# First layer's attention: value pieces traced ahead of transposes and scores

## The chip, the cores and the metric

The kernel runs on one core of a Trainium2 chip. A core has five engines with instruction streams of their own: TensorE (PE; its weight loads are listed apart, as PEld), VectorE (DVE), ScalarE (ACT), GpSimd (POOL) and SyncE (SP), which here issues the DMAs. Each engine runs its instructions in the order in which the program lists them; between engines, semaphores make an instruction wait for what it needs. Matrix products and transposes are written to PSUM, from where DVE and ACT read them; GpSimd works on SBUF only in this kernel.

The metric is the time of one execution on the device, in microseconds (us), as the median of several runs.

## What is computed

Two layers over 1024 latent tokens and 256 context tokens, model width 1024, 16 heads of 64. The first layer is a windowed attention in which four query heads share one key and value head, with rotary embedding and a sink logit per head; the second is a neighbourhood attention on a grid. Both have a gate path. The change lies in the first layer's attention. Cut to what matters:

```python
def block(bi):                       # one block of 128 queries; keys: 3 blocks + context
    s_lat = jnp.einsum('bqkgd,bjkd->bkgqj', qb, kb) * scale
    s_lat = jnp.where(mask, s_lat, NEG_INF)
    s_ctx = jnp.einsum('bqkgd,bckd->bkgqc', qb, kc) * scale
    p = jax.nn.softmax(jnp.concatenate([s_lat, s_ctx, s_sink], axis=-1), axis=-1)
    o = jnp.einsum('bkgqj,bjkd->bqkgd', p_lat, vb) + jnp.einsum('bkgqc,bckd->bqkgd', p_ctx, vc)
    return o.reshape(B, A_BLOCK, A_INNER)
...
y = (o * jax.nn.silu(g)) @ w_out
h = layer_norm(DEEPNORM_ALPHA * h + gate[:, None, :] * y, ln_g[i], ln_b[i])
```

The two context blocks attend to the context alone, and go through the same code with two key tiles instead of four or five.

## The kernel before

**Number format.** Products run on pairs: a value is kept as a high part (a cast) and a low part (the value minus its high part). A projection therefore takes three matmuls (L206 to L208), and the probabilities are stored as `pth` (high) and `ptl` (low).

**Units.** The first layer's attention runs over 8 head pairs `p`, 10 blocks `b` of 128 queries and 2 heads `h`: 160 sub-steps `k`. The two heads of a block form one unit `u`, with sub-steps 2u and 2u+1. Each sub-step has these pieces:

- S, the scores (`qkA`, L692): four matmuls into a PSUM tile "big" (L702, L703). `sm_first` follows: DVE adds the mask and takes the extreme (L315), POOL writes the sink's column (L320), ACT takes the exponential (L322).
- T, the transposes (`trA`, L716, with `sm_transpose`, L329): 2 to 5 transposes of 128 columns into another "big" tile (L334). ACT casts them to `pth` (L338), DVE computes `ptl` (L340). The same piece calls `sm_second` for the next sub-step: DVE's reciprocal (L326) and POOL's scaling (L327).
- V, the values (`pvA_fn`, L723), once per unit and in two halves: V1 multiplies with `pth` of both heads, V2 with `ptl` (L731). After V2 of an odd block the results of two blocks are evacuated: copies on ACT (L740), sums on DVE (L741), the product with the gate on POOL (L744), and at the last block of a pair of heads a store (L748; L746 for the last pair).

**Buffers.** PSUM has two "big" tiles (`psbig`, L95), used by scores and transposes alike, and four "one" tiles (`psone`, L98), used by projections and values. `pth` and `ptl` have two buffers each (`pt_tile`, L342), one per unit.

**Order.** `att_steps` (L750) writes the pieces out row by row. Row k holds T(k), S(k+3), and one half of a unit's values: in odd rows V1 of the unit that ends with sub-step k-2, in even rows V2 of the unit that ends with k-3. So rows 2u+3 and 2u+4 hold V1(u) and V2(u). `merge` (L282) spreads the projections of the gate and of the next head pair's queries between these pieces, in proportion to written costs (545 for T, 545 for S, 1090 / 2 for each half of V), and with a due number for V2 (`needA`, L791), which makes sure that the gate's part is there. Reductions, loads of keys and values, and the column sums of the modulation ("dots", L615, L616, L597) are inserted at fixed places of the list of pieces. For the last head pair the last six pieces are traced after the gates' transposes (L844 to L846).

The order in which pieces are traced is a priority for the planner that orders each engine's instructions; it also goes by when an instruction can be ready by its own estimate. `lift(n)` moves instructions n places ahead: 80 for `sm_first` and `sm_second` (LIFT_A), 60 for L340, 20 for L338. The second layer uses the same `att_steps` with whole value pieces (`split=False`).

Of the kernel before, what the change touches and what calls it, by code (L numbers as in the profile page):

```python
# [80 lines left out]
def build(tc, i, out):  # L81
# [44 lines left out]
    def lift(n):  # L126

        return tc.high_priority(n) if n else nullcontext()
# [196 lines left out]
    def sm_second(s):  # L325
        nc.vector.reciprocal(s.rs, s.sum)  # L326
        nc.gpsimd.tensor_scalar(s.t[:, : s.w], s.t[:, : s.w], s.rs, 1.0, ALU.mult, ALU.mult)  # L327
# [422 lines left out]
    def att_steps(subs, qk, st, tr, pv, last_of_unit, costs, need, ahead, rise, split=False):  # L750

        seq = []
        n = len(subs)
        for k in range(-ahead, n + 2 + split):
            row = []

            def t_piece(k=k):
                if k + 1 < n:
                    with lift(rise(k)):
                        sm_second(st[k + 1])  # L760
                if k >= 0:
                    tr(k)

            def s_piece(k=k):
                qk(k + ahead)

            def v_piece(k=k):
                pv(k - 2)

            def v_first(k=k):  # L770
                pv(k - 2, 0)

            def v_second(k=k):
                pv(k - 3, 1)

            if -1 <= k < n:
                row.append((costs[0] if k >= 0 else 0.0, t_piece, 0))
            if k + ahead < n:
                row.append((costs[1], s_piece, 0))
            if split and 0 <= k - 2 < n and last_of_unit(k - 2):  # L780
                row.append((costs[2] / 2, v_first, 0))
            elif split and k - 3 >= 0 and last_of_unit(k - 3):
                row.append((costs[2] / 2, v_second, need(k - 3, k + ahead)))
            elif not split and k - 2 >= 0 and last_of_unit(k - 2):
                row.append((costs[2], v_piece, need(k - 2, k + ahead)))
            seq.append(row)
        return seq

# [2 lines left out]
    def needA(k, kq):  # L791
# [5 lines left out]
        return G7_AT[c] if p == 7 else 8 * (c + 1)  # L797

    rowsA = att_steps(
        subsA, qkA, stA, trA, lambda k, x: pvA_fn(*subsA[k][:2], x), lambda k: subsA[k][2] == 1,  # L800
        (545, 545, 1090), needA, AHEAD_A, lambda k: LIFT_A, True,
# [6 lines left out]
    for p in range(8):  # L808
# [6 lines left out]
        if p < 7:  # L815
            n = len(att)
# [272 lines left out]
    for p in range(8):  # L1089
# [6 lines left out]
        fillB += gp  # L1096
        g_done.append(len(fillB))
    rowsB = att_steps(
        subsB, qkB, stB, trB, lambda k: pvB_fn(subsB[k][0], subsB[k][1]), lambda k: subsB[k][2] == 1,
        (545, 545, 1310), lambda k, kq: g_done[subsB[k][0] // 2], AHEAD_B, lambda k: LIFT_B if k >= BARE_B else 0,  # L1100
# [86 lines left out]
    for j in range(4):  # L1187
        t = ob.tile([P, D], F32, name=f"vec{j}")
# [136 lines left out]
```

## Time and profile before

| | us |
|---|---|
| median of 3 runs | 1452.0 |
| lowest and highest run | 1451.5, 1457.64 |
| profiled execution | 1452.42 |
| its span | 1450.4 |

The span is the time from the first to the last instruction of the profiled execution; 2.0 us of that execution lie around it. The profile's page lists the busy time of each engine and the chain of work that ended last, followed back from the last instruction. The windows give the busy time of each engine in a stretch of the span. The waits say how long an engine stood still and which instruction ended that. The timeline lists instructions by their start, with the idle time before them in brackets. A matmul's end is modelled, and matmuls overlap, so PE counts as busy where short stalls may hide.

### The profile page before, as it was taken

The page shows a single profiled execution, that of the slowest core. Times are in us where ns is not written, and L with a number is a line of the kernel's source. Part 1 is how long each engine was busy: PE and PEld are TensorE (multiplying, and loading weights), DVE is VectorE, ACT ScalarE, POOL GpSimd, SP SyncE. Part 2 cuts the span into 40 slices and gives each one's busy share as a digit, 9 for nine tenths or more (in the row PEclk, how much of TensorE's full clock was granted, in tenths as well). Part 3 has the DMA queues.
Part 4 walks back from the last instruction along what each step waited for, and adds up shares of the span by engine and source line. Part 5 has one row for each costly group of instructions (what it writes and reads, how often), then busy time and mean ns, then how long its engine had stood idle before and what let it go on. Part 6 is the DMA issues. An engine that isn't in the chain of part 4 may idle for free.

```text
span 1450.4 us, 25150 instructions
## 1 busy us (share of the span) xinstructions
PE 1392.4 (96%) x8816; PEld 1214.8 (84%) x8816; DVE 991.1 (68%) x2220; ACT 733.6 (51%) x1565; POOL 632.2 (44%) x779
## 2 busy tenths in 40 slices
PE   9999999999999999999999999999999999988995
PEld 5887898888888888788898889888988898877774
DVE  4658888878888789566433765555565555677788
ACT  4336776677676777332222545444454445466300
POOL 0326666666666657233301323333233323354664
PEclk9999999999999999999999999999999999999998
DMA  9472114123122124434287565554555464563543
GB/s 370 164 233 83 56 53 131 45 77 101 68 70 62 56 69 130 134 127 141 75 238 227 145 185 171 142 156 151 162 152 171 122 185 137 144 196 97 146 115 93
DMA packets 117229, 195.05 MB, mean 134 GB/s; under 512 B 9328, under 2 KB 57840, under 8 KB 117104
## 3 DMA queue, kind: packets, MB, share of 16 engines
q1 hardware_dynamic: 117104, 193.45, 43.8%
q8 instruction: 70, 1.15, 0.3%
q14 instruction: 55, 0.45, 0.1%
HBM read 141.51 MB, written 51.90 MB: 133 GB/s over the span
## 4 chain that ended last, share of the span: by engine, by line
PE 72%; DVE 11%; DMA 5%; issue 5%; ACT 4%; POOL 3%; SPq 0%; DVEq 0%; ACTq 0%; POOLq 0%
PE pj L207 9%; PE pj L206 9%; PE pj L208 9%; PE T_B L334 4%; PE T_A L334 4%; PE pvB L1064 3%; PE pvA L731 3%; PE pv L240 3%; PE pv L241 3%; PE pv L242 3%; PE S_A L702 2%; PE S_B L1033 2%; PE yA L419 2%; PE yA L418 2%; PE yA L417 2%
## 5 line engine op out<-in xcount | busy, mean ns | idle before, releaser
L327 POOL TENSOR_SCALAR s_B<-s_B,rs_B 128x640 f32<-128x640 f32 (+1 forms) x128 | 102.1, 798 | 305.7 <-DVE rs_B L326 285.6
L206 PE MATMUL pj<-uBh,wh 128*128 128x512 f32 (+1 forms) x448 | 176.2, 393 | 0.0
L207 PE MATMUL pj<-uBl,wh 128*128 128x512 f32 (+1 forms) x448 | 170.1, 380 | 0.0
L208 PE MATMUL pj<-uBh,wl 128*128 128x512 f32 (+1 forms) x448 | 169.8, 379 | 0.0
L322 ACT ACTIVATE s_A<-s_A,m_A 128x641 f32<-128x641 f32 (+2 forms) x160 | 119.5, 747 | 88.6 <-DVE m_A L315 74.3
L322 ACT ACTIVATE s_B<-s_B,m_B 128x640 f32<-128x640 f32 (+1 forms) x128 | 102.9, 804 | 119.9 <-DVE m_B L315 118.9
L340 DVE TENSOR_TENSOR pt_B<-T_B,pt_B 128x640 fp32r<-128x640 f32 (+1 forms) x128 | 100.9, 788 | 81.0 <-ACT pt_B L338 80.4
L162 POOL TENSOR_TENSOR wl<-wr,wh 128x512 fp32r<-128x512 f32 x64 | 87.8, 1372 | 147.7 <-ACT wh L160 143.1
L327 POOL TENSOR_SCALAR s_A<-s_A,rs_A 128x640 f32<-128x640 f32 (+2 forms) x160 | 126.8, 793 | 57.8 <-DVE rs_A L326 55.5
L315 DVE CUSTOM_DVE_ANT_0 s_A<-S_A,msk,nsk 128x640 f32<-128x640 f32 (+2 forms) x160 | 123.5, 774 | 34.0 <-PE S_A L703 17.7
L206 PE MATMUL pj<-uAh,wh 128*128 128x512 f32 (+1 forms) x384 | 140.0, 365 | 0.0
L207 PE MATMUL pj<-uAl,wh 128*128 128x512 f32 (+1 forms) x384 | 137.6, 358 | 0.0
L208 PE MATMUL pj<-uAh,wl 128*128 128x512 f32 (+1 forms) x384 | 137.3, 358 | 0.0
L340 DVE TENSOR_TENSOR ptl_A<-T_A,pth_A 128x640 fp32r<-128x640 f32 (+2 forms) x160 | 114.0, 712 | 15.2 <-PE pvA L731 7.1
L338 ACT CAST pt_B<-T_B 128x640 fp32r<-128x640 f32 (+1 forms) x128 | 84.4, 659 | 67.4 <-PE T_B L334 66.8
L334 PE MATMUL T_A<-ident,s_A 128*128 128x128 f32 x672 | 101.0, 275 | 12.0 <-DVE m_A L315 8.5
L334 PEld LDWEIGHTS T_A<-ident,s_A 128*128 128x128 f32 x672 | 77.2, 140 | 40.0 <-issue 17.0
L315 DVE CUSTOM_DVE_ANT_0 s_B<-S_B,bias 128x640 f32<-128x640 f32 (+1 forms) x128 | 100.3, 784 | 10.7 <-PE S_B L1034 9.7
L338 ACT CAST pth_A<-T_A 128x640 fp32r<-128x640 f32 (+2 forms) x160 | 96.4, 603 | 16.6 <-PE T_A L334 13.8
L334 PE MATMUL T_B<-ident,s_B 128*128 128x128 f32 x608 | 88.2, 274 | 12.5 <-DVE pt_B L340 8.5
L208 PEld LDWEIGHTS pj<-uBh,wl 128*128 128x128 f32 x448 | 84.3, 188 | 16.9
L334 PEld LDWEIGHTS T_B<-ident,s_B 128*128 128x128 f32 x608 | 70.0, 140 | 29.8 <-issue 11.8
(219 smaller groups left out, 3900.1 us busy)
## 6 DMA issues: line engine op xcount, KB each, us to landing
kB<-kdB SPq DMA_DIRECT2D x64, 320.0 KB, 5.3
gw<-in_wadaT SPq DMA_DIRECT2D x48, 256.0 KB, 2.8
vdB<-st SPq DMA_DIRECT2D x20, 512.0 KB, 3.1
vB<-vdB SPq DMA_DIRECT2D x16, 640.0 KB, 5.0
wada<-in_wadaC SPq DMA_DIRECT2D x16, 512.0 KB, 9.6
kdB<-st SPq DMA_DIRECT2D x16, 512.0 KB, 3.0
qdB<-st SPq DMA_DIRECT2D x16, 512.0 KB, 3.7
qB<-qdB SPq DMA_DIRECT2D x32, 256.0 KB, 4.5
```

Of the source, the lines that this page charges most:

```text
L162: e.tensor_tensor(lo, r, f32(hi), ALU.subtract)
L206: mm(pt[:, :n], hi[:, sl], rh, start=kt == 0, stop=False)
L207: mm(pt[:, :n], hi[:, sl], rl, start=False, stop=False)
L208: mm(pt[:, :n], lo[:, sl], rh, start=False, stop=kt == KT - 1)
L240: mm(pt, lh, hi[:, sl], start=kt == 0, stop=False)
L241: mm(pt, lh, lo[:, sl], start=False, stop=False)
L315: nc.vector.tensor_tensor_reduce(outp, sc, in1, scale, init if init is not None else 3e38, ALU.add, ALU.min, accum_out=s.m)
L322: nc.scalar.activation(s.t[:, :n], s.t[:, :n], AF.Exp, bias=s.m, scale=-1.0, accum_out=s.sum)
L327: nc.gpsimd.tensor_scalar(s.t[:, : s.w], s.t[:, : s.w], s.rs, 1.0, ALU.mult, ALU.mult)
L334: nc.tensor.transpose(tp[:, k * P : (k + 1) * P], s.t[:, src * P : (src + 1) * P], ident)
L338: nc.scalar.copy(pt.hi[:, :n, hl, :], tv)
L340: nc.vector.tensor_tensor(pt.lo[:, :n, hl, :], tv, f32(pt.hi[:, :n, hl, :]), ALU.subtract)
```

## The change

In `att_steps` the pieces of a row are collected and put together in another order. With `split` (the first layer) a row with a half of the values now has that half first, then T, then S; before it was T, S, values. Without `split` (the second layer) the order stays T, S, values. Pieces, costs and due numbers are the same.

```diff
-            if -1 <= k < n:
-                row.append((costs[0] if k >= 0 else 0.0, t_piece, 0))
-            if k + ahead < n:
-                row.append((costs[1], s_piece, 0))
+            t = [(costs[0] if k >= 0 else 0.0, t_piece, 0)] if -1 <= k < n else []
+            s = [(costs[1], s_piece, 0)] if k + ahead < n else []
+
             if split and 0 <= k - 2 < n and last_of_unit(k - 2):
-                row.append((costs[2] / 2, v_first, 0))
+                row += [(costs[2] / 2, v_first, 0)] + t + s
             elif split and k - 3 >= 0 and last_of_unit(k - 3):
-                row.append((costs[2] / 2, v_second, need(k - 3, k + ahead)))
+                row += [(costs[2] / 2, v_second, need(k - 3, k + ahead))] + t + s
             elif not split and k - 2 >= 0 and last_of_unit(k - 2):
-                row.append((costs[2], v_piece, need(k - 2, k + ahead)))
+                row += t + s + [(costs[2], v_piece, need(k - 2, k + ahead))]
+            else:
+                row += t + s
             seq.append(row)
```

Over the whole list this exchanges the two halves' places: the sequence T, S, V1, T, S, V2 becomes V1, T, S, V2, T, S, so that the half of a unit stands where the half before it stood.

## The prediction

> **What bounds the kernel now.** I read the page first, then the windows, then the waits of each engine inside the first layer's attention, then the timeline around single waits.
>
> ```profile
> span 1450.4 us, 25150 instructions
> PE 1392.4 (96%) x8816; PEld 1214.8 (84%) x8816; DVE 991.1 (68%) x2220; ACT 733.6 (51%) x1565; POOL 632.2 (44%) x779
> PE 72%; DVE 11%; DMA 5%; issue 5%; ACT 4%; POOL 3%; SPq 0%; DVEq 0%; ACTq 0%; POOLq 0%
> ```
>
> TensorE is busy 96% of the span and is 72% of the chain that ended last. It runs one stream in a fixed order, so time comes back only where that stream stands still. The windows (columns: stretch, its length, then busy us of PE, PEld, DVE, ACT, POOL, clock, DMA share, GB/s) show where that is:
>
> ```profile
> 140.00:590.00 450.00, 432.90 (x2818) 379.36 (x2817) 370.69 (x895) 317.05 (x718) 293.56 (x420) 1.00 0.24 76
> 1000.00:1200.00 200.00, 199.94 (x1362) 183.65 (x1361) 117.39 (x282) 97.24 (x204) 61.60 (x74) 1.00 0.55 159
> ```
>
> The first layer's attention lies in the first stretch: PE is idle 450.00 - 432.90 = 17.1 us there, with DVE at 82% and the clock granted in full. In the second layer PE is idle 0.06 us of 200, so what the first layer gives back should arrive at the end undiminished: the tail is the same PE stream begun earlier. The change can win at most about these 17.1 us, unless stalls are hidden inside matmuls shown as busy. What PE waits for in the attention (window 120 to 600; us in total, times, longest):
>
> ```profile
> PE T_A L334 <- DVE m_A L315: 8.3, 13, 1.6
> PE S_A L702 <- DVE ptl_A L340: 5.1, 7, 1.2
> PE S_A L703 <- DVE ptl_A L340: 1.8, 6, 0.3
> ```
>
> Transposes and scores share two PSUM tiles ("big"). A score waits until L340, the low half of an earlier transpose, has read its tile (6.9 us, 13 times); a transpose waits until L315, the score's reduction, has read its own (8.3 us, 13 times). Both releasers are on DVE.
>
> **The change part by part.** Nothing is added or removed: 80 first and 80 second value pieces, the transposes and the scores stay. In the repeating order T, S, V, T, S, V each value piece takes the place that the previous one had, one step sooner against T and S. What this unties is a buffer. `ptl` has two buffers, a unit is two sub-steps, and unit u+2 takes the buffer of unit u. In row 2u+4 the old order runs T(2u+4), S(2u+7), and only then V2(u), the last reader of that buffer; so L340 of T(2u+4) must wait for a value piece that comes after the next score. In the new order V2(u) precedes T(2u+4). The trace shows the knot (DVE's waits, then the timeline):
>
> ```profile
> DVE ptl_A L340 <- PE pvA L731: 7.1, 14, 1.2
> ```
>
> ```profile
> 299.93 0.71 PE L334 MATMUL T_A<-ident,s_A 128*128 128x128 f32 x5
> ...
> 301.53 0.69 ACT L338 CAST pth_A<-T_A 128x640 fp32r<-128x640 f32 x1
> ...
> 301.77 0.63 PE L731 MATMUL pvA<-ptl_A,vA 128*128 128x256 f32 x4
> ...
> 302.84 0.69 DVE L609 SCALAR_TENSOR_TENSOR gh<-gth,gh 128x512 f32<-128x512 f32 x1 [0.29 <-POOL s_A L327]
> 303.45 0.82 DVE L340 TENSOR_TENSOR ptl_A<-T_A,pth_A 128x640 fp32r<-128x640 f32 x1
> ...
> 303.94 0.69 ACT L338 CAST pth_A<-T_A 128x640 fp32r<-128x640 f32 x1
> ...
> 304.32 0.44 PE L702 MATMUL S_A<-kA,qA 128*128 128x384 f32 x1 [0.53 <-DVE ptl_A L340]
> ...
> 308.51 0.76 PE L731 MATMUL pvA<-ptl_A,vA 128*128 128x256 f32 x5
> ```
>
> The cast that L340 needs ended at 301.53 + 0.69 = 302.22; the value piece ended at 302.40; L340 started at 303.45, behind L609, and the score stood 0.53 us. Without the value piece the planner can put L340 ahead of L609; it would end at about 303.4, before the score's turn at 303.8. The longest such wait has the same shape:
>
> ```profile
> 154.58 0.38 PE L334 MATMUL T_A<-ident,s_A 128*128 128x128 f32 x2
> ...
> 155.44 0.37 ACT L338 CAST pth_A<-T_A 128x256 fp32r<-128x256 f32 x1
> ...
> 156.06 0.93 DVE L470 TENSOR_TENSOR ra<-ra,rb 128x512 f32<-128x512 f32 x1
> 156.10 0.76 PE L731 MATMUL pvA<-ptl_A,vA 128*128 128x256 f32 x5
> ...
> 157.67 1.15 DVE L658 TENSOR_TENSOR qA<-ra,qA 64x512 fp32r<-64x512 f32 x1 [0.28 <-ACT qA L657]
> ...
> 158.85 0.42 DVE L340 TENSOR_TENSOR ptl_A<-T_A,pth_A 128x256 fp32r<-128x256 f32 x1
> ...
> 159.33 0.39 PE L702 MATMUL S_A<-kA,qA 128*128 128x256 f32 x1 [1.20 <-DVE ptl_A L340]
> ```
>
> The cast is over at 155.81, the value piece at 156.86, and L340 comes third on DVE, at 158.85. **Term 1:** 0.53 + 1.20 = 1.7 us back.
>
> The eleven other score waits are 6.9 - 1.7 = 5.2 us. Of L702's seven, five are left with 5.1 - 1.73 = 3.4 us, 0.67 each, and they look like this one:
>
> ```profile
> 338.97 0.76 PE L731 MATMUL pvA<-ptl_A,vA 128*128 128x256 f32 x5
> ...
> 339.92 0.38 ACT L338 CAST pth_A<-T_A 128x256 fp32r<-128x256 f32 x1
> ...
> 340.81 0.69 DVE L658 TENSOR_TENSOR qA<-ra,qA 64x512 fp32r<-64x512 f32 x1
> ...
> 341.53 0.42 DVE L340 TENSOR_TENSOR ptl_A<-T_A,pth_A 128x256 fp32r<-128x256 f32 x1
> ...
> 342.01 0.39 PE L702 MATMUL S_A<-kA,qA 128*128 128x256 f32 x1 [0.67 <-DVE ptl_A L340]
> ```
>
> Here the value piece was over at 339.73 but the cast only at 340.30, and L658 went first on DVE. The buffer did not hold L340 directly; only the order that the planner wrote, perhaps with the buffer in mind, did. The bounds are 0 and 5.2 us. **Term 2:** half, 2.6 us back. The Trainium skill, "Perfetto Trace Analysis", section Optimization Strategy, says that the same gap repeated on the engine that should be saturated can mean too little PSUM or SBUF for the next tile. By it these repeated waits are two PSUM tiles too few, which an order does not cure; the sum would be 2.6 us worse. The trace bears half of that out: they do repeat at 0.67 us, but DVE work of another kind stands between.
>
> The transposes' 8.3 us have mixed causes. One of the larger:
>
> ```profile
> 249.97 1.44 DVE L615 CUSTOM_DVE_ANT_0 gj<-gw,gh 128x512 f32<-128x512 f32 x1 [0.54 <-DMA gw<-in_wadaT]
> ...
> 252.38 0.74 PE L334 MATMUL T_A<-ident,s_A 128*128 128x128 f32 x5 [1.16 <-DVE m_A L315]
> ```
>
> L615, waiting for a load, was ahead of L315. The change does not touch that, but it gives back DVE's 7.1 us of blocked waiting, which now delays whatever is behind L340, L315 among it. The bounds are 0 and 8.3. **Term 3:** a quarter, 2.1 us, since the one shown is of another kind.
>
> What moves along: each second piece of an odd block brings two L740 copies on ACT, two L741 on DVE, the multiply L744 on POOL, and seven times a store on SP's queue:
>
> ```profile
> L741 DVE TENSOR_TENSOR otmp<-pvA,otmp x78: 394/417/420, 138.7 to 591.2; 64x256 f32<-64x256 f32 x78
> L744 POOL TENSOR_TENSOR gA<-otmp,gA x39: 729/737/1227, 141.5 to 591.6; 128x256 f32<-128x256 f32 x39
> L748 SPq DMA_DIRECT2D ogd<-gA x7: 326/327/327, 179.6 to 544.5; - x7
> ```
>
> POOL is busy 293.56 of 450 us and nothing soon reads the stores: cost nothing, covered by POOL's 35% of idle time; uncovered, 0.74 us each. On DVE there is no such cover: if L741 steps in front of L315 just when a transpose needs the tile, it costs 0.42 us each time, between 0 and 40 x 0.42 = 16.7 us (one delay for each of 40 pairs of blocks). L315 is lifted by 80 places and L340 by 60, L741 by none. **Term 4:** near the low end, one such delay, 0.4 us lost.
>
> The new wait: V1(u) now heads row 2u+3 and PE's stream behind it, T and S, waits if the cast of T(2u+1) is late. For the odd transpose whose cast ends at 304.63 the first piece takes the place that now begins at 308.51: 3.9 us of slack. Cost nothing; if casts slipped beyond that, each would hold PE by the excess.
>
> The ends: the last six pieces are traced after the gate transposes. In the new order T(158) falls behind them. Nearest row, the one wait there:
>
> ```profile
> PE yA L417 <- ACT gates L366: 0.9, 1, 0.9
> ```
>
> **Term 5:** between -0.9 and +0.9, taken at 0.4 lost. Sum: 1.7 + 2.6 + 2.1 - 0.4 - 0.4 = 5.6 us. The profiled execution took 1452.42 us, span 1450.4 and 2.0 around it; 1452.4 - 5.6 = **1446.8 us**. The median of the three runs, 1452.0, is 0.4 us below the profiled one, less than any term.
>
> **The rivals.** (a) *More comes back.* Weight loads wait longer for L340 than matmuls do:
>
> ```profile
> PEld S_A L702 <- DVE ptl_A L340: 9.2, 18, 1.4
> PEld S_A L703 <- DVE ptl_A L340: 4.1, 6, 0.7
> ```
>
> If all 9.2 + 4.1 = 13.3 us goes, the time is 1452.4 - 13.3 = 1439.1 us; it lasts only if transposes do not then wait on L315 instead. Against it: some of it is hidden under matmuls still draining. The Trainium skill, "Perfetto Trace Analysis", section Identifying the Most-Contended Engine, calls matmul busy time a bad measure and takes the weight loads' share instead; by it PE has 450 - 379.36 = 70.6 us of room in this stretch, not 17.1. The back-to-back PE rows of the second layer (199.94 of 200) do not settle which is right. (b) *Nothing to measure.* The eleven waits are held by cast and queue, and the transposes' by loads: only Term 1 arrives, 1450.7 us; or the planner, which orders by readiness, already ran the pieces so and nothing changes, 1452.4. (c) *Slower.* The value evacuation, traced ahead, comes before the score's reduction on DVE: L741 in front of L315, the transposes wait 0.42 us at each. All 40 pairs give 16.7 us, less Term 1: 1452.4 + 16.7 - 1.7 = 1467.4. It decides from (7.3 + 1.7) / 0.42 = 21 pairs of 40. For it: DVE is 82% busy and transposes wait for L315 already. Against it: L315 is lifted by hand.
>
> **How the numbers follow.** 0.5% of 1452 is 7.3 us, about what a measurement of this kernel can tell from no change, so faster means below 1444.7 and slower above 1459.3. Forecast (1444.7 to 1450): 0.50. Rival (a): 0.26, all faster. Rival (b): 0.14, all within. Rival (c): 0.10, of which 0.07 beyond 21 pairs and 0.03 within. So faster 0.26, within 0.50 + 0.14 + 0.03 = 0.67, slower 0.07. The range runs from 1439 (rival (a), with the part above that value) to 1456 (rival (c) with 13 pairs: 5.4 - 1.7 = 3.7 us lost); it leaves out perhaps 0.08 on either side.
>
> **What would show it.** Right: DVE's waits of L340 for L731 (7.1 us, 14 times) nearly gone; scores waiting for L340 at 4 us or less from 6.9; transposes' waits for L315 at 6 to 7 us; PE's busy time from 140 to 590 unchanged in kind; span about 1444.8. Rival (b): the first goes and the second stays at 5 us. Rival (a): the second is nil and PE's idle time in the attention falls below 8 us. Rival (c): the transposes' waits for L315 rise past 15 us, with L741 running just ahead of L315. I am wrong altogether if PE waits for the cast L338 at value pieces, or if the second layer, whose trace order stays, loses or wins time of its own.

## The result and the profile after

The changed kernel takes 1462.7 us (median of four runs, 1460.8 to 1466.7) against 1452.0 before: a ratio of 1.0074, 95% interval 1.0058 to 1.0089. It is 10.8 us slower; 1446.8 was forecast. The profiled execution took 1462.72 us, with a span of 1460.9. Ratios here go by the fast runs alone and are not always the quotient of the medians shown (for a_tv0, below, they differ by some 0.001); one slow run of a_s0, at 1527.03 us, is left out of its median.

The page of the changed kernel (busy time of the engines, then the engines' shares of the chain that ended last):

```profile
span 1460.9 us, 25125 instructions
PE 1394.7 (95%) x8815; PEld 1221.4 (84%) x8816; DVE 990.4 (68%) x2220; ACT 734.0 (50%) x1565; POOL 634.3 (43%) x779
PE 62%; DVE 16%; ACT 6%; issue 6%; DMA 5%; POOL 4%; SPq 0%; DVEq 0%; ACTq 0%; POOLq 0%
```

The engines do the same work as before, but DVE has 16% of the chain instead of 11%. The windows of the changed kernel, with the start of the attention first (columns as in the prediction):

```profile
100.00:120.00 20.00, 16.75 (x89) 14.34 (x88) 13.40 (x34) 11.60 (x25) 7.40 (x13) 0.83 0.65 185
140.00:590.00 450.00, 427.18 (x2768) 376.84 (x2767) 366.29 (x887) 312.75 (x709) 293.69 (x419) 1.00 0.24 75
1000.00:1200.00 200.00, 199.94 (x1347) 182.88 (x1346) 118.30 (x284) 97.87 (x204) 62.95 (x74) 1.00 0.55 159
```

and the one of these stretches of the kernel before that has not been shown:

```profile
100.00:120.00 20.00, 19.12 (x119) 16.31 (x119) 13.81 (x33) 11.90 (x26) 8.36 (x13) 1.00 0.69 190
```

Between 140 and 590 PE is busy 427.2 us instead of 432.9, and 2768 matmuls start there instead of 2818. The second layer is untouched, 199.94 us of 200 in both. What PE waits for in the first layer's attention (120 to 610) in the changed kernel:

```profile
PE T_A L334 <- DVE ptl_A L340: 10.3, 15, 3.1
PE T_A L334 <- DVE m_A L315: 4.9, 9, 1.5
PE S_A L702 <- DVE ptl_A L340: 3.1, 3, 1.1
PE pvA L731 <- ACT pth_A L338: 1.7, 3, 0.8
```

The two waits that the prediction spoke of did become smaller: scores for L340 from 6.9 us to 3.1, transposes for L315 from 8.3 to 4.9. In their place stands one that the kernel before does not have at all: transposes that wait for L340, the low half of the transposes *before* them, 10.3 us. The value piece is no longer what L340 waits for. DVE's two longest waits in the changed kernel (120 to 610):

```profile
DVE rs_A L326 <- ACT s_A L322: 38.5, 57, 1.2
DVE ptl_A L340 <- ACT pth_A L338: 24.4, 50, 1.2
```

and the rows for these in the kernel before:

```profile
DVE rs_A L326 <- ACT s_A L322: 21.1, 43, 1.0
...
DVE ptl_A L340 <- ACT pth_A L338: 4.0, 9, 0.7
```

L340 for L731, 7.1 us before, is gone; L340 now comes to its turn early and stands waiting for the cast, six times as long as before. The timeline shows how that reaches PE. This is the change from the first head pair to the second, in the changed kernel; the values are those of the context blocks, the transposes those of block 0 of the next pair:

```profile
168.03 0.63 PE L334 MATMUL T_A<-ident,s_A 128*128 128x128 f32 x4
168.41 0.47 PE L206 MATMUL pj<-uAh,wh 128*128 128x512 f32 x1
...
169.31 0.44 PE L702 MATMUL S_A<-kA,qA 128*128 128x384 f32 x1
169.37 0.83 ACT L322 ACTIVATE s_A<-s_A,m_A 128x641 f32<-128x641 f32 x1 [1.55 <-POOL s_A L320]
...
169.99 0.40 PE L731 MATMUL pvA<-pth_A,vA 128*128 128x256 f32 x2
...
170.32 0.59 ACT L338 CAST pth_A<-T_A 128x512 fp32r<-128x512 f32 x1
...
170.94 0.69 DVE L340 TENSOR_TENSOR ptl_A<-T_A,pth_A 128x512 fp32r<-128x512 f32 x1 [0.45 <-ACT pth_A L338]
...
171.77 0.63 PE L334 MATMUL T_A<-ident,s_A 128*128 128x128 f32 x4 [0.68 <-DVE ptl_A L340]
```

and the same pieces in the kernel before:

```profile
166.74 0.60 PE L334 MATMUL T_A<-ident,s_A 128*128 128x128 f32 x4
166.80 0.83 ACT L322 ACTIVATE s_A<-s_A,m_A 128x641 f32<-128x641 f32 x1 [0.92 <-DVE m_A L315]
167.09 0.42 PE L702 MATMUL S_A<-kA,qA 128*128 128x384 f32 x1
...
167.75 0.59 ACT L338 CAST pth_A<-T_A 128x512 fp32r<-128x512 f32 x1
...
169.11 0.63 PE L334 MATMUL T_A<-ident,s_A 128*128 128x128 f32 x4
...
169.30 0.69 DVE L340 TENSOR_TENSOR ptl_A<-T_A,pth_A 128x512 fp32r<-128x512 f32 x1 [0.33 <-ACT th L275]
```

Before, the next transposes (169.11) start ahead of the L340 of the last ones (169.30): they take a tile that a *score* has left. In the changed kernel they wait for that L340: they take the tile of the last *transposes*. Counted in the programs, 21 of the 160 transposes took their tile over from transposes before the change, 83 after it. And between T and S there now stand projections (168.41 to 169.31), where S followed T at once before.

Nobody meant to move the projections. `merge` deals them out by place in the list, in proportion to the costs summed up so far, and a head pair's list now begins with a value piece instead of a transpose. (What is inserted at fixed places of the list, the column sums and the loads of keys and values, shifts against the pieces too.) Counted in the program as mean matmul time (us) between the pieces:

| | S to V | V to T | T to S |
|---|---|---|---|
| before | 0.51 | 0.65 | 0.18 |
| changed | 0.54 | 0.28 | 0.57 |

The largest single loss, in the changed kernel:

```profile
377.88 0.75 PE L731 MATMUL pvA<-ptl_A,vA 128*128 128x256 f32 x5
...
379.52 0.69 DVE L615 CUSTOM_DVE_ANT_0 gj<-gw,gh 128x512 f32<-128x512 f32 x1 [3.21 <-DMA gw<-in_wadaT]
...
380.77 0.82 DVE L340 TENSOR_TENSOR ptl_A<-T_A,pth_A 128x640 fp32r<-128x640 f32 x1
...
381.75 0.74 PE L334 MATMUL T_A<-ident,s_A 128*128 128x128 f32 x5 [3.12 <-DVE ptl_A L340]
```

Here DVE stands before L615 for a load, L340 is behind it, and the transposes are right behind the value piece with nothing in between.

Against the kernel before, the fifth product with the gate (L744) of the eight head pairs starts 1.1, 1.0, 3.7, 1.9, 7.6, 7.4, 9.8 and 9.9 us later. The loss comes in steps, the largest of them (5.7 us) in the pair with the wait at 381.75. The waits of PE that the profile lists from 120 to 610 rise only from 19.7 us to 22.3; the rest is hidden behind matmuls shown as busy. The starts of PE's matmuls show it. Take the distance from each matmul to the next, less the median distance behind the same kind of matmul in the kernel before, and add this up from the first score to the last value piece: it is 37.6 us before and 48.6 in the changed kernel, which is about the whole loss. Transposes right behind a value piece have 3.5 us of it before and 16.8 after; together with those behind a projection they have 19.0 and 30.2.

### The profile page after: what moved, and what is told of

It reads as the page before. It is cut to its first block, busy times and chain, and to the rows that moved or that the text cites. A ratio compares the mean times of both kernels' runs of the same rounds, so it can differ in the third digit from the quotient of the medians.

```text
span 1460.9 us, 25125 instructions
## 1 busy us (share of the span) xinstructions
PE 1394.7 (95%) x8815; PEld 1221.4 (84%) x8816; DVE 990.4 (68%) x2220; ACT 734.0 (50%) x1565; POOL 634.3 (43%) x779
## 4 chain that ended last, share of the span: by engine, by line
PE 62%; DVE 16%; ACT 6%; issue 6%; DMA 5%; POOL 4%; SPq 0%; DVEq 0%; ACTq 0%; POOLq 0%
PE pj L207 7%; PE pj L206 7%; PE pj L208 7%; PE T_B L334 4%; PE pvB L1065 3%; DVE s_A L315 3%; PE T_A L334 3%; PE pv L240 3%; PE pv L241 3%; PE pv L242 3%; PE S_B L1034 2%; DVE ptl_A L340 2%; PE yA L418 2%; PE yA L417 2%; PE yA L419 2%
## 5 line engine op out<-in xcount | busy, mean ns | idle before, releaser
L327 POOL TENSOR_SCALAR s_B<-s_B,rs_B 128x640 f32<-128x640 f32 (+1 forms) x128 | 102.3, 800 | 304.8 <-DVE rs_B L326 284.9
L340 DVE TENSOR_TENSOR pt_B<-T_B,pt_B 128x640 fp32r<-128x640 f32 (+1 forms) x128 | 100.9, 789 | 81.0 <-ACT pt_B L338 80.4
L206 PE MATMUL pj<-uAh,wh 128*128 128x512 f32 (+1 forms) x384 | 147.0, 383 | 0.0
L327 POOL TENSOR_SCALAR s_A<-s_A,rs_A 128x640 f32<-128x640 f32 (+2 forms) x160 | 124.6, 780 | 49.7 <-DVE rs_A L326 45.4
L340 DVE TENSOR_TENSOR ptl_A<-T_A,pth_A 128x640 fp32r<-128x640 f32 (+2 forms) x160 | 114.1, 713 | 28.2 <-ACT pth_A L338 27.6
L315 DVE CUSTOM_DVE_ANT_0 s_A<-S_A,msk,nsk 128x640 f32<-128x640 f32 (+2 forms) x160 | 123.1, 771 | 13.2 <-PE S_A L703 10.7
L315 DVE CUSTOM_DVE_ANT_0 s_B<-S_B,bias 128x640 f32<-128x640 f32 (+1 forms) x128 | 100.4, 785 | 10.3 <-PE S_B L1035 9.4
```

Source lines behind the costliest of these rows:

```text
L206: mm(pt[:, :n], hi[:, sl], rh, start=kt == 0, stop=False)
L315: nc.vector.tensor_tensor_reduce(outp, sc, in1, scale, init if init is not None else 3e38, ALU.add, ALU.min, accum_out=s.m)
L340: nc.vector.tensor_tensor(pt.lo[:, :n, hl, :], tv, f32(pt.hi[:, :n, hl, :]), ALU.subtract)
```

## The experiments

All ratios are against the kernel before, on the same chip, whose median lay between 1451.9 and 1452.3.

**DVE's order.** In the program L340 stood behind the score reduction L315 of sub-step k+3 for 135 of 160 transposes before, and for 72 after. Was that order the cause? Both kernels were made to have L340 behind that L315:

```diff
-        with lift(60 if a else 0):
-            nc.vector.tensor_tensor(pt.lo[:, :n, hl, :], tv, f32(pt.hi[:, :n, hl, :]), ALU.subtract)
+        def low():
+            with lift(60 if a else 0):
+                return nc.vector.tensor_tensor(pt.lo[:, :n, hl, :], tv, f32(pt.hi[:, :n, hl, :]), ALU.subtract)
+        return low
...
             def s_piece(k=k):
                 qk(k + ahead)
+                if split and k in lowA:
+                    with tc.issue_after(st[k + ahead].red.ins):
+                        lowA.pop(k)()
```

> The changed kernel, with one thing more: on VectorE the low half (L340) of transposes k is queued behind the score reduction (L315) of sub-step k+3, everywhere. The values stay first. Theory Q (the change lets the planner put L340 ahead of the score reduction on VectorE, where it waits for the cast and holds back the reduction): VectorE's idle time before L340 for the cast falls from 24.4 us to under 8, and the time falls by 6 us or more, to 1457 or below. Theory D (VectorE stands in front of loads for the modulation sums): the time stays at 1460 to 1465. Theory V (the values' place in TensorE's stream is itself what costs): it stays at 1460 to 1465.

> The kernel before, with the same rule on VectorE (L340 behind the score reduction of k+3), which already held for 135 of 160 there. Theory Q: little moves, 1449 to 1455. Theory V: as Q; then a_late stays above this one by 8 to 11 us, where theory Q has them within 4 us.

The changed kernel with this order (a_late) took 1462.3 us, ratio 1.007 (1.0055 to 1.0085); the one before (b_late) 1454.5, 1.0016 (1.0006 to 1.0026). DVE's order alone is not the cause, though the two kernels lie 7.8 us apart instead of 10.8: a_late's waits of PE and DVE show the stall under another name (its L707 is L703 of the others).

```profile
PE T_A L334 <- DVE m_A L315: 15.5, 27, 1.4
PE T_A L334 <- POOL s_A L327: 2.2, 3, 0.7
```

```profile
DVE s_A L315 <- PE S_A L707: 31.9, 48, 1.1
```

The transposes now wait 15.5 us for L315, which itself waits for the scores, since the scores come late behind the projections (counted as above, V to T is 0.33 us there and T to S 0.44). Its transposes take over a tile from transposes only 2 times, so this handover is not needed for the loss.

**The loads.** The stall at 381.75 hangs on a load of the modulation weights. These two kernels leave the loads out and form the column sums from other data, so that their outputs have other values there:

```diff
-            dma(t, i["wadaT"][j, :, h * 512 : (h + 1) * 512])
...
-            nc.vector.tensor_tensor_reduce(o, t, gh[0], 0.5, 0.0, ALU.mult, ALU.add, accum_out=acc[:, j, 0:1])
-            nc.gpsimd.tensor_tensor(t, t, gh[1], ALU.mult)
+            nc.vector.tensor_tensor_reduce(o, gh[1], gh[0], 0.5, 0.0, ALU.mult, ALU.add, accum_out=acc[:, j, 0:1])
+            nc.gpsimd.tensor_tensor(t, gh[0], gh[1], ALU.mult)
```

> The changed kernel without the loads of the modulation weights in the first layer's attention: the sums L615 and L616 run on data that is in SBUF already, so the gates, and so the output, are other values. Theory D: the excess over b_noload is under 3 us. Theory Q: the excess remains, 6 to 11 us, less the one stall of 3.1 us at 381.75 and its slower clock, so at least 4 us.

> The kernel before with the same loads left out: the yardstick of a_noload. Both theories: 1446 to 1452, since its two transposes behind such a load lost 1.16 us each.

1459.1 us with the change (1.0047, 1.0032 to 1.0062), 1449.0 without it (0.9979, 0.9969 to 0.999). The excess stays at 10.1 us: the loads are not the cause, though each kernel gains some 3 us without them.

**One half of the values, one stretch of the attention.** Two kernels put only V2 or only V1 ahead, two put both ahead only in the first head pair or only from the second on:

```diff
             if split and 0 <= k - 2 < n and last_of_unit(k - 2):
-                row += [(costs[2] / 2, v_first, 0)] + t + s
+                row += t + s + [(costs[2] / 2, v_first, 0)]        # v2first
...
             elif split and k - 3 >= 0 and last_of_unit(k - 3):
-                row += [(costs[2] / 2, v_second, need(k - 3, k + ahead))] + t + s
+                row += t + s + [(costs[2] / 2, v_second, need(k - 3, k + ahead))]        # v1first
...
+                vv = [(costs[2] / 2, v_first, 0)]        # and v_second in the other row
+                row += vv + t + s if k < 17 else t + s + vv        # v_p0only; v_from_p1: k >= 17
```

> Only the second half of the values (V2) goes ahead of T and S; the first half (V1) stays last in its row. Theory S (V1 traced early takes its PSUM tile 'one' ahead of the next projection chunk, which then cannot run ahead and fill TensorE while the attention's first chain is waiting; most is lost in the first 10 us of the attention and in the slower clock after that): the stretch 100 to 120 has PE busy 19 us again and clock 1.00, and the time is 1450 to 1455. Theory R (the values' place costs about 1 us in each head pair): half of it, 1456 to 1459. The buffer's release is early here, so the forecast's gain of some 3 us should show if it exists: under theory S then 1448 to 1452.

> Only the first half (V1) goes ahead; V2 stays last. Theory S: the stretch 100 to 120 looks as in the changed kernel (PE busy 16.5 us, clock below 0.95), 1457 to 1464. Theory R: 1456 to 1459.

> Values first in the first head pair only (sub-step rows below 17), the old order after that. Theory S: at least half of the loss, 1457 to 1463. Theory R: one eighth, 1452 to 1455.

> The old order in the first head pair, values first from the second on. Theory S: 1452 to 1457. Theory R: seven eighths of the loss, 1459 to 1463.

v2first 1457.1 us (1.0034, 1.0024 to 1.0045), v1first 1469.6 (1.0124, 1.0099 to 1.015), v_p0only 1453.0 (1.0005, 0.9995 to 1.0015), v_from_p1 1461.1 (1.0062, 1.0043 to 1.008). V2 ahead alone, which is all that the buffer needs, loses as well. The first head pair alone costs about 1 us, which its interval does not tell from nothing, though it has a start like that of the changed kernel (PE 17.01 us busy from 100 to 120); the loss comes with the order in the later head pairs. Not all of v_from_p1's is seen in the attention: in its profiled execution the last product with the gate (L744) starts 4.1 us later than before, and the span is 7.5 us longer. The last L744 of the changed kernel starts 9.9 us later and its span is 10.5 us longer.

**Where the projections stand, by the written costs.** The three costs that `merge` goes by are the only edit, in the kernel with the values ahead (a_) and in the one before (b_):

```diff
-        (545, 545, 1090), needA, AHEAD_A, lambda k: LIFT_A, True,
+        (0, 1090, 1090), needA, AHEAD_A, lambda k: LIFT_A, True,        # a_t0, b_t0
...
+        (1090, 0, 1090), ...        # a_s0, b_s0
+        (545, 0, 2180), ...        # a_sv0
+        (0, 545, 2180), ...        # a_tv0
+        (0, 0, 3270), ...        # a_v0
```

> The changed kernel with other costs in the hand-written order: T 0, S 1090, values as before, so that no projection piece is dealt out between T and the next S, and the same sum. In TensorE's program the work between a score and the next transpose rises from a mean of 1.31 us (changed kernel; 1.61 before) to 1.77, by the nominal length of the matmuls listed there. Theory G (the values' move turned the row against the fill: projections went from between S and T to between T and S, and the transpose that takes over the score's PSUM tile is left with too short a cover): the loss is gone, 1447 to 1455. Theory V (values ahead cost by themselves): 1459 to 1465.

> The kernel before with the same costs (cover from S to T 1.68 us instead of 1.61). Theory G: 1449 to 1454, near its old time; the difference between a_t0 and this is what the place of the values is worth with the fill held fixed: 0 to 4 us in favour of a_t0 if the early release of the low half's buffer pays. Theory V: a_t0 is 8 to 11 us above this.

> The kernel before, values last, with the costs turned the other way (T 1090, S 0): projections between T and S, none earned between S and the values. The cover from S to T falls to a mean of 1.24 us, as in the changed kernel, with no value piece moved. Theory G: slower by 5 us or more, 1457 to 1466, with transposes waiting on VectorE 14 us or more in the attention. Theory V: 1449 to 1455.

> Values first, costs T 545, S 0, each value half 1090: projections between the values and T (a mean of 0.78 us by nominal lengths) and between T and S (0.54, as in the changed kernel), none between S and the values. Theory H (projections between T and S bring the score's reduction and the low half together on VectorE, and the planner then hands a transpose the PSUM tile of the transpose before it, 83 of 160 times in the changed kernel against 21 before; with values ahead this costs): 78 such handovers here, 1457 to 1464. Theory P (a transpose right behind a value piece costs; projections between them heal it): 1447 to 1454.

> Values first, costs T 0, S 545, each value half 1090: projections as before the change, 0.58 us between S and the values, 0.76 between the values and T, 0.02 between T and S; 17 handovers from transpose to transpose. Theory H: 1445 to 1450, as a_t0. Theory P: as well, or up to 3 us below a_t0. If both fall it is 1455 or more.

> Values first, costs T 1090, S 0, values as in the changed kernel: nearly all projections between T and S (1.09 us), 0.26 between the values and T; 113 handovers from transpose to transpose. Theory H: slower than the changed kernel, 1464 to 1475. Theory P: as the changed kernel, 1460 to 1465. A third possibility, that only the sum of work between S and T counts (1.2 us here as in b_s0, which took 1453.5): 1452 to 1456.

> Values first, all cost on the values: projections between the values and T (1.3 us) and nowhere else; 25 handovers from transpose to transpose. Theory H: 1445 to 1451. Theory P: the fastest of all, 1442 to 1447.

The outcome of these stands in the table below. a_t0, with the values ahead, is the fastest kernel of the study at 1447.2 us and beats both kernels; the same costs in the old order (b_t0) give 1453.0. Its waits of PE (120 to 610):

```profile
PE S_A L702 <- issue: 4.5, 3, 1.5
PE T_A L334 <- DVE m_A L315: 3.3, 7, 0.7
...
PE S_A L702 <- DVE ptl_A L340: 1.3, 5, 0.3
...
PE T_A L334 <- DVE ptl_A L340: 0.7, 2, 0.5
PE S_A L703 <- DVE ptl_A L340: 0.5, 1, 0.5
```

The new wait is small here, and so is the transposes' wait for L315. The scores' wait for L340 is not. For the three waits that the profile leaves unnamed ("issue"), the program names L340 as what releases the score's tile, and in the timeline each ends 0.10 us behind an L340:

```profile
216.47 0.42 DVE L340 TENSOR_TENSOR ptl_A<-T_A,pth_A 128x256 fp32r<-128x256 f32 x1
...
216.99 0.36 PE L702 MATMUL S_A<-kA,qA 128*128 128x256 f32 x1 [1.49 <-issue]
```

With them the scores wait 6.3 us for L340, against 6.9 before. b_s0 was meant to show that long projections between T and S are the evil by themselves; at 1453.5 it loses nothing that can be measured, so this simple form fell (although its start is a bad one, PE 15.88 us busy from 100 to 120). a_sv0 was meant to fail, by its many tiles handed from transposes to transposes (78), and was fast: so the number of such handovers alone decides nothing either. a_s0 says what else is needed: with little between V and T and much between T and S it loses 5.8 us by the medians, 5.1 by the ratio.

**Where the projections stand, by the cut of the list.** Costs move all gaps at once. These kernels leave the costs alone and cut the lists of the head pairs one piece later (in the changed kernel) or earlier (in the one before), so that each gets the other's deal of projections, from the second head pair on (the pieces inserted at fixed places move along; the written costs leave those where they are):

```diff
-        att = [x for row in rowsA[p * 20 : (p + 1) * 20] for x in row]
+        att = [x for row in rowsA[p * 20 : (p + 1) * 20] for x in row][1 if p else 0 :]        # a_rot
+        if p < 7:
+            att.append(rowsA[(p + 1) * 20][0])
...
+        if p:                                     # b_rot
+            att.insert(0, rowsA[p * 20 - 1][-1])
+        if p < 7:
+            att.pop()
```

> The values ahead as in the changed kernel, but each head pair's list is cut one piece later (the leading value half of a pair's first row goes to the end of the list of the pair before). So the projections come to stand against T, S and V where they stood before the change: counted in the program, S to V 0.57 us, V to T 0.6, T to S 0.2 of projection matmuls (before: 0.51, 0.65, 0.18; changed kernel: 0.54, 0.28, 0.57). This is the premise on which the prediction was worked out. Theory F (the loss is the place of the projections, which the rotated row shifted; the values' move by itself wins): the 5.6 us of the prediction come back, 1446 to 1450 us, ratio 0.996 to 0.9985; transposes' waits for the transposed tile's low half 5 us or less from 11.1. Theory W (the values' move itself costs, the fill only adds to it): 1453 to 1459, ratio 1.001 to 1.005. If it is like the changed kernel, 1461 or more, the place of the projections within the row has nothing to do with it.

> The order before the change, T, S, V, but each head pair's list is cut one piece earlier, so that the projections stand where they stand in the changed kernel: S to V 0.5 us, V to T 0.27, T to S 0.59. Theory F: this alone brings the loss, 1458 to 1468 us, ratio 1.004 to 1.011, since the same fill with the values a step sooner gives 1462.7. Theory W: no loss of its own, 1450 to 1454, ratio within 0.0015 of 1. In between (1455 to 1458) the two parts act only together. Waits of transposes for the low half's tile: 8 us or more by F, 3 or less by W.

> As a_rot (values ahead, projections where they stood before the change), but the first head pair keeps the order T, S, V, so that the attention starts as before the change (in the stretch 100 to 120 PE was busy 19.12 us before, 17.01 in a_rot, 16.75 in the changed kernel). Theory F2 (the values' move wins with the projections in the old places, and the start hides it): the 2.1 us of the start come back on top of a_rot's 1451.7, 1449.6 us or less, ratio 0.997 to 0.9985. Theory N (with the projections in the old places the move is worth nothing): 1451 to 1453, ratio 0.9993 to 1.0007, although the start is busy 19 us again.

a_rot_p1 is a_rot with the order of the kernel before (T, S, values) in the first head pair. The two by two, medians in us with the ratio to before:

| | projections as before the change | projections as after it |
|---|---|---|
| T, S, V | before: 1452.0 | b_rot: 1454.2, 1.0013 (1.0004 to 1.0022) |
| V, T, S | a_rot: 1451.7, 0.9996 (0.9987 to 1.0005) | changed: 1462.7, 1.0074 (1.0058 to 1.0089) |
| V, T, S from the second head pair on | a_rot_p1: 1449.25, 0.9979 (0.9968 to 0.999) | v_from_p1: 1461.1, 1.0062 (1.0043 to 1.008) |

The windows and waits of a_rot_p1:

```profile
100.00:120.00 20.00, 19.48 (x123) 16.72 (x121) 13.80 (x35) 11.04 (x25) 9.04 (x14) 1.00 0.66 187
140.00:590.00 450.00, 431.64 (x2828) 383.26 (x2829) 367.85 (x897) 317.98 (x721) 291.09 (x421) 1.00 0.25 77
```

```profile
PE T_A L334 <- DVE m_A L315: 6.4, 9, 1.6
PE T_A L334 <- DVE ptl_A L340: 3.1, 8, 0.7
...
PE pvA L731 <- ACT pth_A L338: 2.0, 3, 1.2
```

With the projections in their old places the whole loss is gone, by only moving the cut. With the start kept as well, the values' move wins 2.8 us. For b_rot the figures of theory W came true all but exactly (the ratio inside its bounds, time and wait just above), but a_rot took neither the time of W nor that of F: the new places cost the old order only 2.2 us, but the new order 11.0 (1462.7 - 1451.7). The loss is one of the two together. a_rot's eleven runs lie in two groups (five from 1449.3 to 1449.8, six from 1451.7 to 1453.2), so its figure is less firm than the interval looks. With the median of either group, 1449.7 or 1452.9, the 11.0 would be 13.1 or 9.9.

The kernels whose costs or cuts were changed, ordered by the wait of transposes for L340 as the profile lists it (window 120 to 610; gaps counted in the program):

| | order | V to T | T to S | T waits for L340, us | median, us | ratio (95%) |
|---|---|---|---|---|---|---|
| before | T S V | 0.65 | 0.18 | none | 1452.0 | 1 |
| a_t0 | V T S | 0.24 | 0.06 | 0.7 | 1447.2 | 0.9967 (0.9954 to 0.9979) |
| b_s0 | T S V | 0.75 | 0.61 | 1.0 | 1453.5 | 1.0008 (0.9999 to 1.0017) |
| a_v0 | V T S | 1.30 | 0.01 | 1.4 | 1453.5 | 1.0007 (0.9998 to 1.0016) |
| a_tv0 | V T S | 0.76 | 0.02 | 1.7 | 1450.8 | 0.9977 (0.9959 to 0.9996) |
| b_t0 | T S V | 0.60 | 0.11 | 1.9 | 1453.0 | 1.0003 (0.9994 to 1.0012) |
| a_sv0 | V T S | 0.78 | 0.54 | 2.8 | 1448.05 | 0.9975 (0.9958 to 0.9991) |
| a_rot_p1 | V T S | 0.60 | 0.19 | 3.1 | 1449.25 | 0.9979 (0.9968 to 0.999) |
| b_rot | T S V | 0.27 | 0.59 | 3.4 | 1454.2 | 1.0013 (1.0004 to 1.0022) |
| a_rot | V T S | 0.60 | 0.20 | 3.8 | 1451.7 | 0.9996 (0.9987 to 1.0005) |
| a_s0 | V T S | 0.26 | 1.09 | 4.5 | 1458.1 | 1.0035 (1.0023 to 1.0046) |
| changed | V T S | 0.28 | 0.57 | 10.3 | 1462.7 | 1.0074 (1.0058 to 1.0089) |

With up to 3.8 us of this wait no kernel of the table is more than 2.2 us over the one before. With more, all are slow, and so are v_from_p1 (7.9 us), v2first (9.0) and v1first (17.0, the slowest). The wait is a mark and not the cause: a_late has none of it and is as slow as the changed kernel. A mark that holds for a_late too is how late transposes start behind values and projections, whatever they wait for, by the sum of distances above: at least 27.8 us in all the slow kernels (34.6 in a_late), at most 23.1 in all that lie within 2.3 us of the one before or below it. With the values ahead, the wait is long where little stands between V and T *and* much between T and S. Each alone does no harm: a_t0 has the first, a_sv0 the second. The times hold different starts as well: from 100 to 120 PE is busy 19.1 to 19.5 us in the kernel before, a_t0, b_t0, b_rot and a_rot_p1, and 15.9 to 17.1 in the others.

## Why the prediction was wrong

- **What bounds the kernel: right.** In the profiled execution of the changed kernel 9.9 of the 10.5 us by which its span is longer are there by the last product with the gate in the first layer's attention; the second layer all but kept its time.
- **The knot on `ptl` (Terms 1 and 2): right in kind.** L340's wait for V2 vanished. Scores' waits for L340 came to 3.1 us in the changed kernel, within the 4 us named, and to 2.6 in a_rot_p1. Of these the profile puts 2.2 on the reciprocal L326, which a score does not need; L340 stands just ahead of it and is what the program has these scores wait for. The prediction set against this a rule of the Trainium skill, "Perfetto Trace Analysis", section Optimization Strategy, that a repeated gap can mean too few buffers. In a_rot_p1 these waits fell from 6.9 us to 2.6 with the same two tiles, so there the order cured most of them. In a_t0, the fastest kernel, they stayed at 6.3 us; its gain lies elsewhere.
- **Transposes' waits for L315 (Term 3): right by the rows, not by the cause.** 6 to 7 us were named; the rows have 6.4 in a_rot_p1 and 4.9 in the changed kernel. But the profile puts some of these waits on L320, L326 or L327, whichever ended last. Going by what the program has each transpose wait for (waits over 0.2 us, 120 to 610), L315 holds them for 9.5 us before, 6.5 in the changed kernel, where many wait for L340 instead, 10.5 in a_rot_p1 and 5.5 in a_t0. So on its own premise Term 3 gave nothing back.
- **Term 4 and rival (c): not what happened.** Rival (c) priced the case at 1467.4, near the result, but its sign was transposes waiting for L315 past 15 us, behind L741. That wait fell, so the nearness is chance. Rivals (a) and (b) would have ended below or level with the kernel before.
- **Term 5: harmless.** The wait of L417 for the gates (0.9 us) is gone, and the last transposes wait 0.3 us for them.
- **The wait of V1 for the cast: costed at nothing, 1.7 us in the changed kernel** (2.0 in a_rot_p1). The prediction called this wait a sign of being wrong altogether. It did come, but a_rot_p1 has as much of it and is faster than before, so it is not what lost the time.
- **The step that failed** is the first of the second part: "Nothing is added or removed" and "In the repeating order T, S, V, T, S, V each value piece takes the place that the previous one had, one step sooner against T and S." That holds for the values. It took for granted that the projections between the pieces stay where they were. They are dealt out by place in a list, whose first piece the change made another one: V to T fell from 0.65 us to 0.28, T to S rose from 0.18 to 0.57. With this, transposes take their tile over from transposes 83 times instead of 21, and the longest wait for L340 is that of the transposes and no longer that of the scores. a_rot, which makes the premise true from the second head pair on, takes the loss away.
- **The start** was not in the sum. In the changed kernel fewer projections run there (89 matmuls start from 100 to 120, 119 before), and PE stands while POOL scales the first probabilities. This too goes with the deal of the projections and not with the order alone: a_t0 has the values ahead and PE busy 19.12 us in this stretch, b_s0 has the old order and 15.88. From the timeline of the changed kernel:

```profile
105.31 0.66 PE L334 MATMUL T_A<-ident,s_A 128*128 128x128 f32 x4 [1.86 <-POOL s_A L327]
```

This costs 2.5 us by a_rot against a_rot_p1, 1.1 by v_p0only against before (not told from nothing) and 1.6 by the changed kernel against v_from_p1.
- **The sum on its own premise** was 5.6 us; a_rot_p1 measures 2.8 (1.5 to 4.6 by its interval). Terms 1 and 2 came as forecast there (6.9 us to 2.6 is 4.3). Term 3 did not come (9.5 to 10.5), and waits that the sum had at nothing did: transposes for L340 (3.1 us) and values for the cast (2.0). All waits that the profile lists from 120 to 610 come to 20.3 us there, 19.7 before, so they do not show the gain; the sum of distances between starts does (37.6 us before, 34.7 in a_rot_p1). With other places for the projections the move is worth 5.8 us (b_t0 to a_t0, though their gaps differ too) and 5.4 (b_s0 to a_sv0, with nearly equal gaps).

So the 10.8 us are, by the medians from before to changed over a_rot_p1 and a_rot: 2.8 won, 2.5 lost at the start, and 11.0 lost by the place of the projections in the new order. How the loss splits between the last two is loose by a_rot's two groups: 0.4 and 13.1 by the one, 3.6 and 9.9 by the other.

**What stays open:** why little between V and T and much between T and S are harmless singly and costly together. The tile passed from transposes to transposes, as at 171.77, is seen in the trace, but a_sv0 has 78 such handovers, about as much PE work across them as the changed kernel (2.4 us, counted in the program), and no loss; a_late has 2 and loses as much. Nor is it shown why the fastest kernel, a_t0, wins what it does. A third `ptl` buffer or a third "big" tile was not tried.

Nor do the waits that the profile names show the loss in one place. PE's busy time is a poor witness: a_rot_p1 is 2.8 us faster than before with *less* of it (431.64 against 432.90). The Trainium skill, "Perfetto Trace Analysis", section Identifying the Most-Contended Engine, says to go by MFU (the matmuls' work against the peak) and the weight loads' busy share instead. The weight loads rank these three rightly: 376.84 us in the changed kernel, 379.36 before, 383.26 in a_rot_p1. But the 70.6 us of room that it seemed to give are far from what any kernel found.

## What to carry to other kernels

Where filler work is dealt out by position in a list, moving one piece moves all the filler: list what stands between the pieces before and after, and move the filler back before judging the move. When a wait on a buffer is untied, ask who takes over that buffer next; here the wait went from the scores to the transposes. If a reordering that should win loses, shift the deal of the filler before dropping it: the same order went from 1462.7 to 1447.2 us by two numbers in a list of costs.

## What was not expected of the hardware

A stall costs more than itself. After the wait of 3.12 us at 381.75 the granted clock of the changed kernel fell by half:

```profile
380.00:382.00 2.00, 0.25 (x3) 0.28 (x4) 1.94 (x6) 0.00 (x0) 1.70 (x2) 1.00 0.01 4
382.00:384.00 2.00, 2.00 (x11) 1.79 (x10) 0.56 (x3) 1.48 (x4) 1.43 (x4) 0.68 0.00 0
384.00:386.00 2.00, 2.00 (x7) 1.71 (x7) 1.34 (x3) 0.98 (x4) 0.54 (x1) 0.50 0.08 19
386.00:388.00 2.00, 2.00 (x15) 1.88 (x15) 0.54 (x3) 1.28 (x3) 0.72 (x2) 0.96 0.32 112
```

From 382 to 388 it lost 2 x (0.32 + 0.50 + 0.04) = 1.7 us of full clock, with PE shown as fully busy. The start did the same: its waits of 0.61, 1.86 and 0.77 us between 102 and 108 went with a clock of 0.83 from 100 to 120, 3.4 us of full clock, where the kernel before had 1.00.

```profile
106.00:108.00 2.00, 1.23 (x7) 0.85 (x7) 1.37 (x2) 1.63 (x3) 0.83 (x2) 0.56 0.73 161
108.00:110.00 2.00, 2.00 (x10) 1.97 (x9) 1.52 (x5) 1.41 (x3) 0.18 (x1) 0.50 0.10 25
```

All twenty kernels of the study divide this way: where PE is busy 19.1 us or more from 100 to 120 the clock is 1.00, and where it is busy 17.1 us or less the clock is 0.83 or 0.91. None lies between. The Trainium skill, "TensorE: Matmul & The Clock Gate", Part 1, has the clock halved after an idle window of about 3.4 us. The single wait of 3.12 us agrees roughly with that; the start of the changed kernel, whose longest wait is 1.86 us, reached half speed with PE still busy 2.8 of the 6 us.
